# Combining attention parts inside the mixing stage, giving slabs back behind the evacuation, rounding T4 on GpSimd

## The chip, the cores and the metric

The kernel runs on one core of a Trainium2 chip. That core has a matrix engine (TensorE, PE in the profile), a vector engine (VectorE, DVE), an activation engine (ScalarE, ACT), a general engine (GpSimd, POOL) and a queue that issues transfers (SyncE, SP). Each engine works through its own instructions in order, and waits on semaphores for the others. The metric is the device time of one execution in microseconds; a kernel's time is the median of its runs.

## The reference

One layer of a hybrid encoder with 1024 channels runs on two batches of 512 tokens, in float32:

```python
xn = rmsnorm(x, norm1_g)
lru_x, lru_gate, q, k, v, gates = split(xn @ w_in)
xc = dwconv(lru_x); h = rglru(xc, forward) + rglru(xc, backward)
a_out = (gelu(lru_gate) * h) @ w_lru_out
# q, k: rmsnorm per head and rope; three groups of 8 heads, windows 128, 512, 2048, dilations 1, 4, 16
wts = softmax(lse of the three groups); o = sum(wts * out of the three groups)
b_out = o @ w_att_out
x = x + (sig(g_a) * a_out + sig(g_b) * b_out) @ w_o
up = rmsnorm(x, norm2_g) @ w_up;  gate, val = split(up)
x = x + (gelu(dwconv(gate)) * val) @ w_down
```

There are 1280 recurrent channels (10 tiles of 128), 512 columns of attention output after the groups are combined, and 3072 feed-forward channels (24 tiles, called f).

## The kernel before, in words

**Products.** Every float32 operand is split into a rounded part hi and a remainder lo, and each product is three matmuls (hi by hi, hi by lo, lo by hi) of 128x128 weights against 512 columns, `mm3`. Activations stay transposed in SBUF.

**The weight stream.** The weights of the whole program are one list of slabs, `specs`, in the order of use. An object `ws` moves along it at two points: SP loads a raw slab (128x512, four buffers `raw`), and `split_to` (L221 to L232) makes hi (ACT or DVE, L226 and L228) and lo (L231, on the engines of the list `lo_eng` in turn; V is DVE, G is POOL) in rings of eight. `ws.take` hands slabs to a product, `ws.done` gives their ring places back, `ws.adv(n)` writes the loads and splits of the next n slabs at that place of the program. Since each engine runs in order, the place of `ws.done` and `ws.adv` sets what stands ahead of what on ACT, DVE, POOL and SP. `defer(n, fn)` writes work n steps later.

**Stages**, in us of the profiled execution: norms and transposes; the first stage (to 424), columns of w_in for the recurrence (L), the output gates (G, stored as tanh in `sg_d`) and the first three gate columns (Y), with the recurrence's small blocks (`lru_slot`) in between; projections and attention (to about 1025), whose parts for 128 tokens and a head group go out to `num_d` with their maxima and sums; the other gate columns (to 1083), seven columns with two halves of 24 matmuls, each multiplied by the recurrence's h into y; the mixing of batch 0 (to 1179), the output product, the mixing and output product of batch 1, the second norm and the operands of a Strassen-Winograd form of the up product (to about 1390); up products (to 1848); down products (to the end).

**Combining.** Eight parts t of 128 tokens are combined, each from three groups. `comb_load` (L858) loads three 128x528 tiles, `combine` (L866) takes 13 operations of 128x8 on DVE, one exp on ACT (L874, with an activation table to load when the gelu's was there), three 128x512 multiplications on DVE (L883) and two additions on POOL (L885, L886). Parts 0 to 3 (batch 0) are transposed by PE (`o_transpose`, L891 to L898; L895 is the matmul); parts 4 to 7 (batch 1) go to DRAM `o_d`, stored from POOL's queue (L888), and are read again in the output product of batch 0. Before, all eight are combined in the gate columns i = 2 to 6 by the table `combs` (L914), up to two per column.

**Mixing.** `mix_tile` (L1002) makes one of eight output tiles of 128 channels: 30 matmuls of y and 12 of the attention output into a pair of PSUM banks, two pairs in turn. Its epilogue on DVE reads the halves with the gates tha and thb (L1018, L1019; `th_load` L994 loads them a tile ahead), adds them (L1020), and makes hi on ACT (L1021) and lo on DVE (L1022).

**Feed-forward.** The seven products of a tile f use operands B11, B21, T2, T1, T3, B22, T4. `batch0` (L1222) makes the first two; its results are copied to p1 (ACT, L1229) and added to g0 (DVE, L1234). `rest` (L1237) makes the other five in banks A and C: u (ACT copy L1248, or for f < 4 a DVE add L1246), p5 (ACT L1253 or DVE L1251), then T3, B22 and T4 continue in the same banks. `prod` (L1207, its matmuls L1214 to L1216) ends with `ws.done` and `ws.adv`, so the next slabs' loads, sums (DVE, L260) and splits are written ahead of the evacuation of this product. The operands T1 to T4 of batch 1 are made in four parts of 128 tokens by `sums_T` (L1130 to L1168): for T4 POOL makes two sums (L1145 is the helper's line), ACT rounds (L1166), POOL makes the remainder.

Of the kernel before, what the change touches and what calls it, by code (L numbers as in the profile page):

```python
# [11 lines left out]
F32 = mybir.dt.float32  # L12
F32R = mybir.dt.float32r
AF = mybir.ActivationFunctionType
ALU = mybir.AluOpType
# [99 lines left out]
def layer_kernel(ctx: ExitStack, tc: tile.TileContext, xs_in, norm1_g, w_in, conv_w, conv_b, lru_wa, lru_ba,  # L115
# [468 lines left out]
    for s, (typ, c) in enumerate(steps1):  # L584
        if s < 2:
            continue
        slabs = ws.take(2)
        ps = ps1.tile([128, 2, 512], F32, tag="m", bufs=2, name="ps")
# [33 lines left out]
    cm_a, ap = open_pool("att", side="right")  # L622
    lo_eng[0] = G

# [240 lines left out]

    def combine(t, cg):  # L866
        d = p3.tile([128, 3, 8], F32, tag="cd", bufs=2, name="cd")
        e = p3.tile([128, 3, 8], F32, tag="ce", bufs=2, name="ce")
        m = p3.tile([128, 8], F32, tag="cm", bufs=2, name="cm")
        V.tensor_tensor(out=m, in0=cg[0][:, 512:520], in1=cg[1][:, 512:520], op=ALU.max)  # L870
# [15 lines left out]
        G.tensor_tensor(out=cg[0][:, 0:512], in0=cg[0][:, 0:512], in1=cg[2][:, 0:512], op=ALU.add)  # L886
        if t >= 4:
            defer(1, lambda: G.dma_start(out=o_d[128 * (t - 4):128 * (t - 4) + 128, :], in_=cg[0][:, 0:512]))  # L888
        else:
            defer(1, lambda: o_transpose(t, cg[0], ps2, "tr"))  # L890
# [22 lines left out]
    ATT_DONE = 3  # L913
    combs = {2: (0,), 3: (1, 2), 4: (3, 4), 5: (5, 6), 6: (7,)}  # L914
    h_load(EARLY_Y)
# [156 lines left out]
    def o_phase(b, hook, orders):  # L1072
        for n, (kq, hlf) in enumerate(orders):
# [5 lines left out]
            ws.done("a", 4)  # L1079

    th_load(0, 0)
    ws.adv(8)
    for c in range(KD):
        mix_tile(0, c)
        if c == 3:
            load_acc(0)
            SP.dma_start(out=gain2, in_=norm2_g[0].partition_broadcast(128))
# [47 lines left out]
    def sums_T(i, pst):  # L1135
# [29 lines left out]
        yield  # L1165
        A.copy(out=hi("T4"), in_=t1)  # L1166
        sub(G, lo("T4"), t1, hi("T4"))
# [38 lines left out]

    def prod(ps, slab, op, start, free=True):  # L1207

        wh, wl = slab
        bh, bl = x2[op]  # L1210
        for k in range(4):
            a = wh[:, 128 * k:128 * k + 128]
            kw = dict(skip_group_check=True)
            PE.matmul(out=ps, lhsT=a, rhs=bh[:, k], start=(start and k == 0), stop=False, **kw)  # L1214
            PE.matmul(out=ps, lhsT=a, rhs=bl[:, k], start=False, stop=False, **kw)  # L1215
            PE.matmul(out=ps, lhsT=wl[:, 128 * k:128 * k + 128], rhs=bh[:, k], start=False, stop=(k == 3), **kw)  # L1216
        if free:
            ws.done("a", 1)
            ws.adv(pace[0])

# [3 lines left out]
    def batch0(f, nm="A", mid=None):  # L1224
# [3 lines left out]
        p1[f] = row("p1", 2)  # L1228
        A.copy(out=p1[f], in_=pa)  # L1229
        if mid:  # L1230
            mid()
        prod(pb, ws.take(1)[0], "B21", True)
        g0s[f] = row("g0", EARLY)
        V.tensor_tensor(out=g0s[f], in0=p1[f], in1=pb, op=ALU.add)  # L1234
        return pa

    def rest(f, pa, mid=None):  # L1237
# [9 lines left out]
        else:  # L1247
            A.copy(out=u2, in_=pa)  # L1248
        prod(pc, ws.take(1)[0], "T1", True)
        if early:  # L1250
            V.tensor_tensor(out=p5, in0=p1[f], in1=pc, op=ALU.add)  # L1251
        else:
            A.copy(out=p5, in_=pc)  # L1253
        prod(pa, ws.take(1)[0], "T3", False)
        if mid:
            mid()
        V.tensor_tensor(out=p5, in0=p5, in1=pa, op=ALU.add)
        prod(pc, ws.take(1)[0], "B22", False)
        V.tensor_tensor(out=u2, in0=u2, in1=pc, op=ALU.add)
        w = lambda j: vff[:, 24 * j + f:24 * j + f + 1]  # L1260
        gc = fp.tile([128, 2, S], F32, tag="gc", bufs=1, name="gc")
# [6 lines left out]
        act(out=gc, in_=gc, func=AF.Gelu_apprx_tanh)  # L1268
        prod(pa, ws.take(1)[0], "T4", False)
        V.tensor_tensor(out=gc[:, 1], in0=gc[:, 1], in1=p5, op=ALU.mult)  # L1270
        if early:
# [126 lines left out]
```

## Time and profile before

| | before |
| --- | --- |
| times, two runs | 2118.45 and 2120.14 us, median 2119.3 |
| profiled execution | 2119.48 us, span 2117.7, so 1.8 us lie around the span |
| PE busy | 2028.3 us, 96% of the span |
| DVE, ACT, POOL busy | 1320.9, 878.3, 669.1 us |
| granted TensorE clock, mean | 0.984 |
| DMA | 220.28 MB, mean 104 GB/s |

Times below are microseconds from the start of the span. A granted clock of 1.00 is 2.4 GHz, 0.50 is 1.2 GHz; a value between is a mixture over the stretch. In a row of a timeline the bracket tells how long the engine idled before it and which instruction ended that; several equal instructions in a row are one line with their number.

### The profile page before, as it was taken

Reading aid. Unit: us, or ns where it says so; the run is one execution under the profiler, and the core shown is the slowest. Engines: PE = TensorE matmul, PEld = TensorE weight load, DVE = VectorE, ACT = ScalarE, POOL = GpSimd, SP = SyncE. Lnnn points to the kernel's source line nnn. Section 1 sums busy time; section 2 is a strip of 40 time slices with the busy share of each in tenths; the row PEclk is TensorE's granted clock in tenths of the full one; section 3 lists DMA queues with packets and bytes.
Section 4 is the critical chain, followed back from the end, with each engine's and each line's share of the span. In section 5 each row is a group of like instructions: output and inputs, shape, how many; then the busy total and the mean of one; then the engine's idle time right before and its main releaser. Section 6 shows DMA issues by size and latency. Waiting matters only on the chain. (4 is left out here: it accounts for less than half of the span.)

```text
span 2117.7 us, 26439 instructions
## 1 busy us (share of the span) xinstructions
PE 2028.3 (96%) x9571; PEld 1708.6 (81%) x9571; DVE 1320.9 (62%) x1896; ACT 878.3 (41%) x1503; POOL 669.1 (32%) x562
## 2 busy tenths in 40 slices
PE   8999999899999999999979999877999999999999
PEld 6877777688899999998767888666888888788887
DVE  5589988736881673366675564666655555465555
ACT  4478888831442143125533332433444444421210
POOL 3111111025211522423343133442445544532421
PEclk9999999999999999999999999989999999999999
DMA  4444545431111111103547565312223332352322
GB/s 146 143 130 121 143 129 160 122 107 46 31 41 46 43 42 58 44 14 96 171 130 237 162 187 169 124 50 90 81 69 90 90 90 71 128 199 80 110 90 80
DMA packets 203776, 220.28 MB, mean 104 GB/s; under 512 B 28892, under 2 KB 148222, under 8 KB 203646
## 3 DMA queue, kind: packets, MB, share of 16 engines
q1 hardware_dynamic: 201278, 212.30, 32.4%
q0 software_dynamic: 2368, 6.29, 1.2%
q8 instruction: 75, 1.23, 0.2%
q14 instruction: 55, 0.45, 0.1%
HBM read 162.51 MB, written 50.79 MB: 101 GB/s over the span
## 5 line engine op out<-in xcount | busy, mean ns | idle before, releaser
L231 POOL TENSOR_TENSOR lo<-raw,hi 128x512 fp32r<-128x512 f32 (+1 forms) x252 | 344.1, 1377 | 661.8 <-ACT hi L228 559.7
L228 ACT CAST hi<-raw 128x512 fp32r<-128x512 f32 (+1 forms) x352 | 205.0, 606 | 322.6 <-PE psd L1351 152.8
L816 PE MATMUL ps<-hi,xh 128*128 128x512 f32 x576 | 252.3, 438 | 5.5 <-ACT gl L602 5.5
L817 PE MATMUL ps<-lo,xh 128*128 128x512 f32 x576 | 229.2, 398 | 0.0
L818 PE MATMUL ps<-hi,xl 128*128 128x512 f32 x576 | 228.8, 397 | 0.0
L152 PE MATMUL ps<-xh,hi 128*128 128x512 f32 x544 | 216.1, 397 | 0.3 <-DVE xc L404 0.3
L153 PE MATMUL ps<-xl,hi 128*128 128x512 f32 x544 | 214.0, 393 | 0.0
L154 PE MATMUL ps<-xh,lo 128*128 128x512 f32 x544 | 213.7, 393 | 0.0
L1352 DVE TENSOR_TENSOR accd<-accd,psd 128x512 f32<-128x512 f32 x192 | 130.0, 685 | 109.5 <-PE psd L1351 104.2
L816 PEld LDWEIGHTS ps<-hi,xh 128*128 128x128 f32 x576 | 156.6, 272 | 15.8 <-ACT gl L602 5.9
L817 PEld LDWEIGHTS ps<-lo,xh 128*128 128x128 f32 x576 | 158.8, 276 | 6.0
L818 PEld LDWEIGHTS ps<-hi,xl 128*128 128x128 f32 x576 | 156.8, 272 | 8.1
L1351 PE MATMUL psd<-hi,hp 128*128 128x512 f32 x384 | 149.4, 389 | 0.0
L1350 PE MATMUL psd<-lo,hp 128*128 128x512 f32 x384 | 149.4, 389 | 0.0
L1349 PE MATMUL psd<-hi,hp 128*128 128x512 f32 x384 | 149.4, 389 | 0.0
L716 ACT ACTIVATE p<-p,nm 128x128 f32<-128x128 f32 (+1 forms) x192 | 81.7, 427 | 144.2 <-DVE nm L714 143.8
L1214 PE MATMUL pfA<-T,hi 128*128 128x512 f32 x288 | 115.2, 400 | 19.1 <-ACT u L1248 14.1
L152 PEld LDWEIGHTS ps<-xh,hi 128*128 128x128 f32 x544 | 103.7, 191 | 23.9 <-issue 0.9
L638 DVE TENSOR_REDUCE ss<-sq 128x8 f32<-128x512 f32 x48 | 32.9, 685 | 142.4 <-ACT sq L635 142.4
L154 PEld LDWEIGHTS ps<-xh,lo 128*128 128x128 f32 x544 | 103.4, 190 | 22.4
L153 PEld LDWEIGHTS ps<-xl,hi 128*128 128x128 f32 x544 | 103.9, 191 | 21.5
L1216 PE MATMUL pfA<-T,lo 128*128 128x512 f32 x288 | 114.8, 399 | 0.9 <-POOL lo L231 0.9
(267 smaller groups left out, 4544.4 us busy)
## 6 DMA issues: line engine op xcount, KB each, us to landing
raw<-in_w_in_dram SPq DMA_DIRECT2D x144, 256.0 KB
raw<-in_w_up_dram SPq DMA_DIRECT2D x56, 256.0 KB
r<-in_w_up_dram SPq DMA_DIRECT2D x48, 256.0 KB
f_d<-gc SPq DMA_DIRECT2D x24, 512.0 KB
raw<-in_w_down_dram SPq DMA_DIRECT2D x48, 256.0 KB
hraw<-f_d SPq DMA_DIRECT2D x24, 512.0 KB
sg_d<-sgt SPq DMA_DIRECT2D x16, 512.0 KB
raw<-in_w_lru_out_dram SPq DMA_DIRECT2D x32, 256.0 KB
```

The lines of the kernel that those rows point to most:

```text
L152: PE.matmul(out=ps, lhsT=a, rhs=b, start=(k == 0), stop=False)
L153: PE.matmul(out=ps, lhsT=a, rhs=rl(k), start=False, stop=False)
L154: PE.matmul(out=ps, lhsT=wl(k), rhs=b, start=False, stop=(k == n - 1))
L228: A.copy(out=hi[:, 0:n], in_=r[:, 0:n])
L231: e.tensor_tensor(out=lo[:, 0:n], in0=r[:, 0:n], in1=hi[:, 0:n], op=ALU.subtract)
L816: PE.matmul(out=ps, lhsT=a, rhs=hi, start=(k == 0), stop=False)
L817: PE.matmul(out=ps, lhsT=a, rhs=lo, start=False, stop=False)
L818: PE.matmul(out=ps, lhsT=b, rhs=hi, start=False, stop=(k == KD - 1))
L1349: PE.matmul(out=ps, lhsT=hh[:, i, tl], rhs=w[0], start=(i == 0), stop=False)
L1350: PE.matmul(out=ps, lhsT=hh[:, i, tl], rhs=w[1], start=False, stop=False)
L1351: PE.matmul(out=ps, lhsT=hl[:, i, tl], rhs=w[0], start=False, stop=(i == 1))
L1352: V.tensor_tensor(out=acc[t][:, cl], in0=acc[t][:, cl], in1=ps, op=ALU.add)
```

## The change

It has four edits. The parts 4 to 7 are combined after tiles 1 to 4 of batch 0's mixing, in tiles called late that use the space of the norm's later operands; their loads stand on SP behind the gate loads of tiles 0 and 1, and their stores to `o_d` are issued by SP one tile after the combining. The parts 0 to 3 are combined one per gate column. In the feed-forward products `ws.done` and `ws.adv` are now a function `give`, called behind each product's evacuation. T4's rounding goes from ACT to POOL. In the last five steps of the first stage `lo_eng` alternates between DVE and POOL where it was DVE alone.

```diff
@@ -584,6 +584,8 @@
     for s, (typ, c) in enumerate(steps1):
         if s < 2:
             continue
+        if s == len(steps1) - 5:
+            lo_eng[:] = [V, G]
         slabs = ws.take(2)
         ps = ps1.tile([128, 2, 512], F32, tag="m", bufs=2, name="ps")
         main_mm(ps[:, 0], 0, slabs)
@@ -620,7 +622,7 @@
     cm_sb, ring_pool["b"] = open_pool("slabs_b")
     ws.open_ring("b")
     cm_a, ap = open_pool("att", side="right")
-    lo_eng[0] = G
+    lo_eng[:] = [G]
 
     msk = ap.tile([128, 768], F32, name="msk")
     rope = ap.tile([128, 12, 2, 16], F32, name="rope")
@@ -863,10 +865,10 @@
             cg.append(c)
         return cg
 
-    def combine(t, cg):
-        d = p3.tile([128, 3, 8], F32, tag="cd", bufs=2, name="cd")
-        e = p3.tile([128, 3, 8], F32, tag="ce", bufs=2, name="ce")
-        m = p3.tile([128, 8], F32, tag="cm", bufs=2, name="cm")
+    def combine(t, cg, small=None):
+        d, e, m = small or (p3.tile([128, 3, 8], F32, tag="cd", bufs=2, name="cd"),
+                            p3.tile([128, 3, 8], F32, tag="ce", bufs=2, name="ce"),
+                            p3.tile([128, 8], F32, tag="cm", bufs=2, name="cm"))
         V.tensor_tensor(out=m, in0=cg[0][:, 512:520], in1=cg[1][:, 512:520], op=ALU.max)
         V.tensor_tensor(out=m, in0=m, in1=cg[2][:, 512:520], op=ALU.max)
         for g in range(3):
@@ -884,9 +886,7 @@
                             op=ALU.mult)
         G.tensor_tensor(out=cg[0][:, 0:512], in0=cg[0][:, 0:512], in1=cg[1][:, 0:512], op=ALU.add)
         G.tensor_tensor(out=cg[0][:, 0:512], in0=cg[0][:, 0:512], in1=cg[2][:, 0:512], op=ALU.add)
-        if t >= 4:
-            defer(1, lambda: G.dma_start(out=o_d[128 * (t - 4):128 * (t - 4) + 128, :], in_=cg[0][:, 0:512]))
-        else:
+        if t < 4:
             defer(1, lambda: o_transpose(t, cg[0], ps2, "tr"))
 
     def o_transpose(t, src, pool, tag):
@@ -911,7 +911,7 @@
             hts[c, b] = t
 
     ATT_DONE = 3
-    combs = {2: (0,), 3: (1, 2), 4: (3, 4), 5: (5, 6), 6: (7,)}
+    combs = {2: (0,), 3: (1,), 4: (2,), 5: (3,)}
     h_load(EARLY_Y)
     for c in range(EARLY_Y, KR):
         i = c - EARLY_Y
@@ -1078,10 +1078,28 @@
                 hook(4 * n + i, i if n == 3 else None)
             ws.done("a", 4)
 
+    late = {}
+
+    def late_load(t):
+
+        r = x20p.tile([128, 2048], F32, name="late", tag=("B11h", "B11l", "B21h", "B21l")[t - 4], bufs=1)
+        cg = [r[:, 528 * g:528 * g + 528] for g in range(3)]
+        for g in range(3):
+            SP.dma_start(out=cg[g], in_=num_d[g][128 * t:128 * t + 128, :])
+        r3 = lambda ap: ap.rearrange("p (g h) -> p g h", g=3)
+        late[t] = cg, (r3(r[:, 1584:1608]), r3(r[:, 1608:1632]), r[:, 1632:1640])
+
     th_load(0, 0)
     ws.adv(8)
     for c in range(KD):
         mix_tile(0, c)
+        if c in (0, 1):
+            late_load(4 + 2 * c)
+            late_load(5 + 2 * c)
+        if 1 <= c <= 4:
+            combine(c + 3, *late[c + 3])
+        if 2 <= c <= 5:
+            SP.dma_start(out=o_d[128 * (c - 2):128 * (c - 2) + 128, :], in_=late[c + 2][0][0][:, 0:512])
         if c == 3:
             load_acc(0)
             SP.dma_start(out=gain2, in_=norm2_g[0].partition_broadcast(128))
@@ -1163,7 +1181,7 @@
         sub(G, t1, hi("B21"), t2)
         sub(G, t1, t1, lo("B21"), ALU.add)
         yield
-        A.copy(out=hi("T4"), in_=t1)
+        G.tensor_scalar(out=hi("T4"), in0=t1, scalar1=1.0, scalar2=1.0, op0=ALU.mult, op1=ALU.mult)
         sub(G, lo("T4"), t1, hi("T4"))
         yield
 
@@ -1204,7 +1222,11 @@
     g0s, p1 = {}, {}
     pace = [1]
 
-    def prod(ps, slab, op, start, free=True):
+    def give():
+        ws.done("a", 1)
+        ws.adv(pace[0])
+
+    def prod(ps, slab, op, start):
 
         wh, wl = slab
         bh, bl = x2[op]
@@ -1214,9 +1236,6 @@
             PE.matmul(out=ps, lhsT=a, rhs=bh[:, k], start=(start and k == 0), stop=False, **kw)
             PE.matmul(out=ps, lhsT=a, rhs=bl[:, k], start=False, stop=False, **kw)
             PE.matmul(out=ps, lhsT=wl[:, 128 * k:128 * k + 128], rhs=bh[:, k], start=False, stop=(k == 3), **kw)
-        if free:
-            ws.done("a", 1)
-            ws.adv(pace[0])
 
     bank = lambda nm: pf[nm].tile([128, 512], F32, tag=nm, bufs=2, name="pf" + nm)
     row = lambda nm, bufs=1: fp.tile([128, S], F32, tag=nm, bufs=bufs, name=nm)
@@ -1227,11 +1246,13 @@
         prod(pa, ws.take(1)[0], "B11", True)
         p1[f] = row("p1", 2)
         A.copy(out=p1[f], in_=pa)
+        give()
         if mid:
             mid()
         prod(pb, ws.take(1)[0], "B21", True)
         g0s[f] = row("g0", EARLY)
         V.tensor_tensor(out=g0s[f], in0=p1[f], in1=pb, op=ALU.add)
+        give()
         return pa
 
     def rest(f, pa, mid=None):
@@ -1246,17 +1267,21 @@
             V.tensor_tensor(out=u2, in0=p1[f], in1=pa, op=ALU.add)
         else:
             A.copy(out=u2, in_=pa)
+        give()
         prod(pc, ws.take(1)[0], "T1", True)
         if early:
             V.tensor_tensor(out=p5, in0=p1[f], in1=pc, op=ALU.add)
         else:
             A.copy(out=p5, in_=pc)
+        give()
         prod(pa, ws.take(1)[0], "T3", False)
         if mid:
             mid()
         V.tensor_tensor(out=p5, in0=p5, in1=pa, op=ALU.add)
+        give()
         prod(pc, ws.take(1)[0], "B22", False)
         V.tensor_tensor(out=u2, in0=u2, in1=pc, op=ALU.add)
+        give()
         w = lambda j: vff[:, 24 * j + f:24 * j + f + 1]
         gc = fp.tile([128, 2, S], F32, tag="gc", bufs=1, name="gc")
         for b, g in enumerate((g0s.pop(f), u2)):
@@ -1267,6 +1292,7 @@
                                    op0=ALU.mult, op1=ALU.add)
         act(out=gc, in_=gc, func=AF.Gelu_apprx_tanh)
         prod(pa, ws.take(1)[0], "T4", False)
+        give()
         V.tensor_tensor(out=gc[:, 1], in0=gc[:, 1], in1=p5, op=ALU.mult)
         if early:
             V.tensor_tensor(out=p5, in0=p1[f], in1=pa, op=ALU.add)
```

Three places show how the instructions move. Line numbers of the changed kernel are larger, from L864 on by 2, in the feed-forward by some 20. A name's ending counts the buffers.

SP's queue, from the weights of one mixing tile to the next (`raw` are weights, `tha` and `thb` the gates, `num_d` the parts in DRAM), at the gates of tile 1, before:

```order
L217 DMA raw<-in_w_att_out_dram 128x4x128
L217 DMA raw<-in_w_lru_out_dram 128x4x128 x2
L217 DMA raw<-in_w_lru_out_dram 128x2x128
L998 DMA tha<-sg_d 128x512
L998 DMA thb<-sg_d 128x512
L217 DMA raw<-in_w_att_out_dram 128x4x128
L217 DMA raw<-in_w_lru_out_dram 128x4x128 x2
L217 DMA raw<-in_w_lru_out_dram 128x2x128
L998 DMA tha<-sg_d 128x512
```

The same place now:

```order
L217 DMA raw<-in_w_att_out_dram 128x4x128
L217 DMA raw<-in_w_lru_out_dram 128x4x128 x2
L217 DMA raw<-in_w_lru_out_dram 128x2x128
L998 DMA tha<-sg_d 128x512
L998 DMA thb<-sg_d 128x512
L1088 DMA late<-num_d_63 128x528
L1088 DMA late<-num_d_64 128x528
L1088 DMA late<-num_d_65 128x528
L1088 DMA late<-num_d_63 128x528
L1088 DMA late<-num_d_64 128x528
L1088 DMA late<-num_d_65 128x528
L217 DMA raw<-in_w_att_out_dram 128x4x128
```

Six loads of late parts now stand between the gates of tile 1 and the weights behind them; six more stand behind the gates of tile 2.

DVE, in the mixing of batch 0, from one tile's epilogue (L1018 to L1022) over the remainders of the next weights (L231) to the next epilogue, before:

```order
L1018 SCALAR_TENSOR_TENSOR tha<-tha,ps 128x512
L1019 SCALAR_TENSOR_TENSOR thb<-thb,ps 128x512
L1020 TENSOR_TENSOR tha<-tha,thb 128x512
L1022 SCALAR_TENSOR_TENSOR ml<-tha,mh 128x512
L231 TENSOR_TENSOR lo<-raw,hi 128x512
L231 TENSOR_TENSOR lo<-raw,hi 128x256
L1018 SCALAR_TENSOR_TENSOR tha<-tha,ps 128x512
L1019 SCALAR_TENSOR_TENSOR thb<-thb,ps 128x512
```

Now, between the epilogue of tile 1 and that of tile 2, from the sum of the weights of a part to the first instructions of tile 2's epilogue (L883 and L885 are L881 and L883 of before; five rows of 128x8 operations stand ahead of these):

```order
L880 TENSOR_TENSOR late<-late 128x8
L881 RECIPROCAL late<-late 128x8
L883 TENSOR_TENSOR late<-late 128x8
L885 TENSOR_TENSOR late<-late 128x512
L883 TENSOR_TENSOR late<-late 128x8
L885 TENSOR_TENSOR late<-late 128x512
L883 TENSOR_TENSOR late<-late 128x8
L885 TENSOR_TENSOR late<-late 128x512
L231 TENSOR_TENSOR lo<-raw,hi 128x512
L231 TENSOR_TENSOR lo<-raw,hi 128x256
L1018 SCALAR_TENSOR_TENSOR tha<-tha,ps 128x512
L1019 SCALAR_TENSOR_TENSOR thb<-thb,ps 128x512
```

One whole part has moved in ahead of the weights' remainders and of the next tile's epilogue; so it is behind tiles 1 to 4.

ACT, around the copy u of f = 0 (L1248; `s` and `r` are sums and slabs of the up weights), before:

```order
L228 CAST hi<-r_11452 128x512
L228 CAST hi<-raw 128x512
L1166 CAST T_11016<-acc 128x4x128 x3
L228 CAST hi<-r_11454 128x512
L1248 COPY u_11670<-pfA 128x512
L228 CAST hi<-s_11702 128x512
L1253 COPY p_11671<-pfC 128x512
L228 CAST hi<-s_11701 128x512
```

The same place now (the copy is L1269, the copy of p5 L1275):

```order
L228 CAST hi<-r_11432 128x512
L228 CAST hi<-raw 128x512
L1269 COPY u_11650<-pfA 128x512
L228 CAST hi<-r_11434 128x512
L1275 COPY p_11651<-pfC 128x512
L228 CAST hi<-s_11683 128x512
L228 CAST hi<-s_11682 128x512
```

Three roundings of T4 (L1166) stood ahead of the copy and are gone from ACT, and each copy now stands ahead of the hi of the slab that its product gives way to.

## Rows read from the trace of the kernel before

**Rows 1.** Windows: busy us (instructions) per engine, granted clock, DMA share, GB/s
```profile
1040.00:1087.00 47.00, 36.05 (x157) 28.70 (x155) 38.27 (x97) 23.73 (x34) 19.62 (x14) 0.96 0.44 130
1087.00:1117.00 30.00, 21.02 (x85) 17.09 (x86) 21.68 (x46) 8.24 (x14) 14.17 (x13) 0.84 0.50 159
1117.00:1136.00 19.00, 19.00 (x77) 15.52 (x77) 12.83 (x16) 7.76 (x15) 7.81 (x6) 0.90 0.71 221
1155.00:1175.00 20.00, 20.00 (x90) 16.57 (x89) 8.63 (x13) 6.01 (x10) 5.18 (x4) 1.00 0.52 161
1390.00:1410.00 20.00, 11.84 (x40) 9.23 (x39) 9.82 (x9) 5.67 (x11) 13.80 (x10) 0.73 0.14 41
1510.00:1840.00 330.00, 330.00 (x1457) 273.27 (x1456) 181.68 (x224) 140.89 (x228) 168.68 (x123) 1.00 0.28 86
```

**Rows 2.** Waits of PE, 1000 to 1490 us: total, times, longest
```profile
PE pt L895 <- POOL cg L886: 8.0, 4, 3.3
PE pfB L1214 <- DVE g L1234: 4.8, 1, 4.8
...
PE pfC L1214 <- DVE p L1251: 2.7, 1, 2.7
PE pfA L1214 <- DVE u L1246: 2.4, 2, 1.5
```

**Rows 3.** Timeline of PE, columns and mixing: start, us, instruction, [idle <-releaser]
```profile
1060.91 0.66 PE L895 MATMUL pt<-ident,cg 128*128 128x128 f32 x4 [2.50 <-POOL cg L886]
...
1070.30 1.11 PE L895 MATMUL pt<-ident,cg 128*128 128x128 f32 x4 [3.26 <-POOL cg L886]
...
1087.18 0.80 PE L152 MATMUL ps<-yh,hi 128*128 128x512 f32 x1 [4.01 <-ACT gl L957]
...
1116.68 0.76 PE L152 MATMUL ps<-yh,hi 128*128 128x512 f32 x1 [8.80 <-DVE thb L1019]
```

**Rows 4.** Timeline of SP's queue before the third mixing tile
```profile
1112.50 0.32 SPq L998 DMA_DIRECT2D thb<-sg_d  x1
```

**Rows 5.** Timeline of DVE, one combining of attention parts
```profile
1044.98 0.15 DVE L870 TENSOR_TENSOR cm<-cg 128x8 f32<-128x8 f32 x1
...
1047.90 0.69 DVE L883 TENSOR_TENSOR cg<-cg,cd 128x512 f32<-128x512 f32 x1
...
1048.70 1.80 DVE L883 TENSOR_TENSOR cg<-cg,cd 128x512 f32<-128x512 f32 x1
```

**Rows 6.** Timeline of POOL, the same combining
```profile
1048.67 1.28 POOL L885 TENSOR_TENSOR cg<-cg 128x512 f32<-128x512 f32 x1 [5.36 <-DVE cd L881]
1050.64 1.59 POOL L886 TENSOR_TENSOR cg<-cg 128x512 f32<-128x512 f32 x1 [0.68 <-POOL cg L885]
```

**Rows 7.** Timeline of ACT, operand T4 and the first u copy
```profile
1395.99 0.62 ACT L1166 CAST T<-acc 128x512 fp32r<-128x512 f32 x1 [5.42 <-POOL acc L1145]
1400.55 0.62 ACT L1166 CAST T<-acc 128x512 fp32r<-128x512 f32 x1 [3.93 <-POOL acc L1145]
...
1401.59 0.58 ACT L1248 COPY u<-pfA 128x512 f32<-128x512 f32 x1
```

**Rows 8.** Timeline of PE: T3(0), the end of T4(0), T3(4)
```profile
1402.22 0.80 PE L1214 MATMUL pfA<-T,hi 128*128 128x512 f32 x1 [8.16 <-ACT u L1248]
...
1412.80 0.39 PE L1216 MATMUL pfA<-T,lo 128*128 128x512 f32 x1
...
1477.13 0.80 PE L1214 MATMUL pfA<-T,hi 128*128 128x512 f32 x1 [5.93 <-ACT u L1248]
```

**Rows 9.** Timeline of POOL, the last T4 remainder
```profile
1401.24 1.26 POOL L1145 TENSOR_TENSOR T<-acc,T 128x512 fp32r<-128x512 f32 x1 [0.73 <-ACT T L1166]
```

**Rows 10.** Groups of POOL by line and shape, whole span
```profile
L436 POOL TENSOR_SCALAR x<-xc 80x1024 fp32r<-80x1024 f32 x16 | 21.7, 1356 | 155.6 <-DMA xc<-xc_d 134.2 <-PE psg L458 21.5
```

**Rows 11.** Waits of PE, 380 to 440 us
```profile
PE ps L816 <- ACT gl L602: 5.5, 1, 5.5
PE psg L457 <- DVE u L468: 4.0, 1, 4.0
```

## The prediction, made before the changed kernel ran

> **What bounds the kernel now.** I read the windows first. From 1510 to 1840 us TensorE (PE) is busy for all of 330 us with 1457 recorded matmuls, 0.2265 us each at a granted clock of 1.00 [rows 1]: there nothing that another engine does sooner can help. So the change can only win where PE idles, or where it works at the lower of its two clock levels after idling. The list of PE's waits and its timeline say where those places are [rows 2, 3], at the mixing, in the first feed-forward products and at the end of the first stage; all that the change touches lies in them. Three edits concern this: **A**, four of the eight attention parts are combined during batch 0's mixing and not before it; **B and D**, the first feed-forward products (slabs given back behind the evacuation; T4 rounded by GpSimd, which is POOL); **C**, six lo subtractions go from VectorE (DVE) to POOL at the end of the first stage.
>
> **A, what goes.** Between the gate columns PE waits for POOL's last add of a part, four times, 8.0 us in all, of which 2.50 and 3.26 are the later two [rows 2, 3]. Then it waits 4.01 us for the last gate column and 8.80 us before the third mixing tile. This last one is a queue's: tile 0's second PSUM half can't be read until thb has been loaded, and SP issues that load only at 1112.50 [rows 4], since its wait is for a store of a combined part from POOL's queue. After the change DVE does one part per column, so the two later waits, the 4.01 and that store are gone: 2.50 + 3.26 + 4.01 + 8.80 = 18.6 us. The 8.0 − 2.50 − 3.26 = 2.2 us of the first two waits I leave, since those columns still have a part each. The idle stretches also cost clock. The clock of 0.84 over 1087 to 1117 and 0.90 over 1117 to 1136 [rows 1] is time at the lower level: 0.10 / 0.5 x 19 = 3.8 us of it in the second window, where PE is busy throughout, so half of that, 1.9, is lost; behind the 3.26 and the 4.01 waits the matmul rows at 1070.30 and 1087.18 are long (1.11 and 0.80 us), and the first window's 0.96 makes 0.04 / 0.5 x 47 = 3.8 us; some 2.6 us of work at half rate behind each wait lose 1.3 each. Sum for A: 18.6 + 4.5 = 23 us.
>
> **A, what it adds.** Each of mixing tiles 1 to 4 gets a part on DVE. One part holds DVE from 1044.98 to 1048.70 + 1.80 = 1050.50, 5.5 us [rows 5]. Without parts a tile takes DVE 8.63 us in 20 us (1155 to 1175), in the window with more to catch up 12.83 in 19 [rows 1]; a tile is 42 matmuls, 42 x 0.2265 = 9.5 us, so 4.1 to 6.4 us. Together 9.6 to 11.9 us of DVE in tiles of 9.5: over four tiles DVE falls behind by 0.4 to 9.6 us. PE feels it only when a PSUM pair isn't read in time: two pairs, so tile c + 2 starts a tile later, less the two reads, 0.7 us each by an operation of that shape [rows 5], 8.1 us of room. Stall 0 to 1.5 us; I take 0, as the mean of the two ends, 5, is inside the room. The twelve loads (128 x 528 x 4 bytes, 3.2 MB) stand on SP behind the gates of the next tile and ahead of its weights; the DMA share there was 0.50 to 0.71 [rows 1], so I take them as hidden by the slabs split ahead, with 0 to 4 us as bounds. The four POOL adds take 1.28 to 1.59 us [rows 6] with two lo subtractions behind them.
>
> The last multiplication of that part took 1.80 us where the one ahead of it took 0.69, and it ran while POOL's add ran [rows 5, 6]. The Trainium skill, "SBUF — State Buffer", section "SBUF: two separate sides", calls the pair of ports that DVE and GpSimd share an exclusive lock, held for a whole instruction; this pair of rows agrees, and no run here yet shows it in the mixing stage. By that rule every POOL instruction could stop one DVE instruction in full; the second rival works that out from rows.
>
> **B and D, the first f.** T3 of f = 0 starts 8.16 us late, in a stretch where PE works 11.84 of 20 us at a clock of 0.73 [rows 1], because the copy u leaves ACT only at 1401.59 [rows 7, 8]. ACT works in order, and ahead of that copy stand T4's roundings, which waited 5.42 and 3.93 us for POOL. D takes the roundings off ACT, so u is copied as soon as T2 ends. Late next is POOL: T4's last remainder ended at 1401.24 + 1.26 = 1402.50 [rows 9]. Two waits for ACT of 0.73 go, three roundings come at 0.68 each (half of 1.356 us for 1024 columns [rows 10]; up to 1.28, a two-operand add, if POOL has no better rate), and POOL meets DVE's T sums more, for which I take 1.8 us, one and a half operations delayed by 1.1 to 1.3 us each as in [rows 5]: 1402.50 − 1.46 + 2.04 + 1.8 = 1404.9. One lo (1.28) stands behind it for T4's slab: 1406.2. T4(0) then ends after 2.72 us and about 1.4 us of lower clock at 1410.4, against 1412.80 + 0.23 = 1413.0 before [rows 8]: **2.6 us** won of the 8.16. Bounds: 0 (POOL's chain 2.6 longer) to 8.16 + 2.7 (it is no bound at all, and T3's half rate, 0.80 us in its first row, goes as well).
> The wait of 4.8 us for g, at f = 3's first products, [rows 2] gets longer by about 1 us, since POOL's T4 work collides with DVE ahead of it. The waits on p (2.7) and u (2.4) at f = 2 and 3 [rows 2] are waits for DVE additions that stood behind the next slab's sums and lo; with B the addition comes first. I count 2.7 and the longer u wait (1.5) less 0.8 of a read still due, 3.4 us. At f = 4 T3 waits 5.93 us for u and then runs at half rate (0.80 us first row [rows 8]), 2.7 us lost: 8.6 us. The copy u now stands ahead of the next slabs' hi, but still behind one hi that waits for a load, and p behind two, so I leave 4.4 us: 4.2 won. From f = 5 on PE is full [rows 1] and the reordering is worth 0; its cover is PE's own work, with two PSUM banks per name. If a slab's lo came too late there, it would show as idle PE. One late evacuation near 1846 may give 0.8. Sum for B and D: 2.6 − 1 + 3.4 + 4.2 + 0.8 = **10 us**, bounds 1 and 18.
>
> **C.** PE waits 4.0 us for u and 5.5 for gl around the end of the first stage [rows 11]. DVE loses six subtractions of about 0.7 us there (0.69 for that shape [rows 5]), but the chain that ends last runs through the last blocks and the last gelu, of which I take a fifth of the 5.5: 1.2 us, bounds +1 (POOL's 1.28 us delays a slab) and −3.
>
> **The sum.** 23 + 10 + 1.2 = 34.2 us. The profiled execution took 2119.48 us (span 2117.7), 0.2 above the median of 2119.3: 2119.5 − 34.2 = **2085 us**. About 2%, 42 us, is what a measurement can tell from no change: under 2077 is faster by that, over 2162 slower.
>
> **Rivals.**
> *POOL is not in the way* (0.18): roundings and sums don't collide, the first f wins its bound, C its 3 and the two small column waits go too: 34 + 8 + 1.8 + 2.2 = 46 less 34.2, so 12 more: **2073**. For: ACT's waits of 5.42 and 3.93 were waits for POOL alone [rows 7]. Against: it is POOL's chain all the same.
> *DVE bounds the mixing* (0.18): POOL has two adds and two lo per tile; if each holds a DVE operation back by 1.1 us (1.80 − 0.69), the tile costs DVE 10.1 + 4.4 = 14.5 us, 5 over the tile, 20 in four, less 8 of room: 12 us stall, **2097**. The lock rule of that Trainium skill page would bring this.
> *T4 only changes the engine waited for* (0.05): B and D win 1, not 10: **2094**.
> *Slower* (0.04): SP holds it back. The weights of tile c + 2 stand behind loads and stores of the late parts, and their buffers come free only when POOL's lo, queued behind the two adds, is done. If a part ends more than one tile (9.5 us) after its tile's epilogue, each of tiles 2 to 5 stops as the third tile did: 8.80 plus about 5 of lower clock, 4 x 13.8 = 55: **2140**. Against: 1.5 us of stall at most by the rows above.
> The forecast's own case, 2078 to 2093, has 0.55. The range of 2066 to 2106 takes in the first two rivals with their bounds. Faster by over 2%: 0.2, from the first rival and the edge of the forecast; within 2%: 0.77; slower by over 2%: 0.03, the far end of the last rival.
>
> **What the profile will show.** Right: mixing starts near 1076, its third tile near 1095 without a gap; T3(0) follows T1 without a wait, and T4(0) waits 3 to 6 us for POOL; 1510 to 1840 stays full. Wrong: PE waits for DVE's thb operation or POOL's lo between tiles 2 and 6 (second or last rival), no wait at T4(0) (first), idle PE in the later f (B costs something).

## The result, and the profile after

The changed kernel took 2095.8 us (2095.2 and 2096.45), before 2119.3: a ratio of 0.9889 with a 95% interval of 0.9847 to 0.9932, 23.5 us faster. The forecast was 2085 with a range of 2066 to 2106. The time lies inside the range, 11 us above the forecast, outside the forecast's own case of 2078 to 2093 and between the rivals at 2094 and 2097. The profiled execution's span is 2093.4 us, 24.3 less than before.

Where the 24.3 us went shows in the starts of the stages. Each number is the start of the first matmul of that stage in PE's timeline, in us; a stage's length is the difference between two columns.

| kernel | projections | mixing, batch 0 | output product | mixing, batch 1 | feed-forward | down | end |
| --- | --- | --- | --- | --- | --- | --- | --- |
| before | 424.2 | 1087.2 | 1175.8 | 1225.6 | 1351.6 | 1852.6 | 2117.7 |
| the change | 427.2 | 1077.9 | 1156.5 | 1209.5 | 1335.7 | 1827.1 | 2093.4 |
| change in the stage ahead | +3.0 | -12.3 | -10.0 | +3.2 | +0.2 | -9.6 | +1.2 |

So A is worth 12.3 + 10.0 - 3.2 - 0.2 = 18.9 us (the forecast had 23), the feed-forward 9.6 less 1.2 given back in the down products (10), and the first stage, where C is, became 3.0 us longer (1.2 shorter). These are two single profiles; how far such starts scatter is said at the experiments.

PE's waits of the changed kernel between 1030 and 1480 us (total, times, longest), which answer to [rows 2, 3, 8]:

```profile
PE pfB L1236 <- DVE g L1254: 6.5, 1, 6.5
PE pt L895 <- DMA ost<-o_d: 3.5, 2, 3.3
PE pfA L1236 <- POOL T L1184: 2.7, 1, 2.7
PE pfA L1236 <- ACT u L1269: 2.5, 1, 2.5
PE pt L895 <- POOL cg L888: 2.2, 2, 1.3
PE ps L152 <- DVE thb L1019: 2.1, 1, 2.1
```

The 4.01 and 8.80 us before and in the mixing, the later two waits for a part, and the 8.16 us at T3(0) are gone. Three waits are new or longer: 2.1 at the eighth and last mixing tile (tile 7, as tiles are numbered from 0; the expectations below call it the seventh), 3.3 for the load of a part into its tile ost, and 6.5 for g, which was 4.8. T4 now waits for POOL (2.7, with 0.9 and 0.9 more in its first matmuls).

Windows of the changed kernel, with the columns of [rows 1]: the last gate columns, the four mixing tiles with a part, the start of the output product, the first feed-forward products, the later ones:

```profile
1054.00:1078.00 24.00, 23.23 (x109) 19.33 (x110) 17.61 (x43) 12.29 (x19) 12.80 (x10) 1.00 0.40 124
...
1097.00:1145.00 48.00, 47.84 (x212) 39.29 (x210) 40.65 (x92) 13.24 (x26) 20.76 (x15) 1.00 0.65 217
1145.00:1170.00 25.00, 19.62 (x89) 15.83 (x90) 18.46 (x23) 8.36 (x15) 8.31 (x7) 1.00 0.69 221
1380.00:1400.00 20.00, 15.46 (x57) 11.56 (x56) 13.41 (x12) 7.57 (x11) 14.48 (x11) 0.83 0.11 35
1500.00:1810.00 310.00, 310.00 (x1369) 256.86 (x1368) 190.46 (x213) 131.71 (x212) 162.73 (x113) 1.00 0.27 82
```

From 1054 to 1145 PE has its full clock and hardly idles. DVE is busy 40.65 of 48 us in the tiles with parts. From 1500 on PE is as full as before: the reordering neither won nor cost there.

DVE's timeline of one tile with a part, from the epilogue's last operation (L1022) of tile 1 to that of tile 2, and POOL's beside it:

```profile
1100.34 0.69 DVE L1022 SCALAR_TENSOR_TENSOR ml<-tha,mh 128x512 fp32r<-128x512 f32 x1 [0.70 <-ACT mh L1021]
...
1103.87 0.69 DVE L885 TENSOR_TENSOR late<-late 128x512 f32<-128x512 f32 x1
...
1104.68 1.80 DVE L885 TENSOR_TENSOR late<-late 128x512 f32<-128x512 f32 x1
1106.40 2.12 DVE L231 TENSOR_TENSOR lo<-raw,hi 128x512 fp32r<-128x512 f32 x2
...
1109.75 1.72 DVE L1020 TENSOR_TENSOR tha<-tha,thb 128x512 f32<-128x512 f32 x1
1112.17 0.69 DVE L1022 SCALAR_TENSOR_TENSOR ml<-tha,mh 128x512 fp32r<-128x512 f32 x1 [0.70 <-ACT mh L1021]
```

```profile
1104.65 1.28 POOL L887 TENSOR_TENSOR late<-late 128x512 f32<-128x512 f32 x1 [5.56 <-DVE late L883]
1106.61 1.62 POOL L888 TENSOR_TENSOR late<-late 128x512 f32<-128x512 f32 x1 [0.68 <-PE ps L153]
1108.20 2.72 POOL L231 TENSOR_TENSOR lo<-raw,hi 128x512 fp32r<-128x512 f32 x2
```

A tile takes DVE 1112.17 - 1100.34 = 11.83 us, against PE's 9.5, at the upper end of the 9.6 to 11.9 of the prediction. Three operations in it are long: the third multiplication (1.80, not 0.69), a remainder of half the width inside the 2.12, and the sum L1020 (1.72). Each begins beside one of POOL's. The whole trace of the kernel before shows the same pair: 366 of DVE's TENSOR_TENSOR operations of 128x512 read two operands in SBUF; the 246 that began with no arithmetic of POOL running took 0.70 us at most, and of the 120 that began beside one 116 took over 0.80. Another 468 of that shape read one operand from PSUM; 148 of them began beside POOL, and none took over 0.70. Then the lag adds up. The eighth tile stops, and later the output product waits for the first part of batch 1, whose load SP issues only at 1160.43, behind weight loads that wait for buffers. PE's two stops, and SP's queue:

```profile
1146.91 0.47 PE L152 MATMUL ps<-yh,hi 128*128 128x512 f32 x1 [2.08 <-DVE thb L1019]
...
1165.47 0.66 PE L895 MATMUL pt<-ident,ost 128*128 128x128 f32 x4 [3.35 <-DMA ost<-o_d]
```

```profile
1156.37 3.54 SPq L219 DMA_DIRECT2D raw<-in_w_o_dram  x4
1159.95 0.42 SPq L1115 DMA_DIRECT2D yst<-y_d  x1
1160.43 0.42 SPq L1118 DMA_DIRECT2D ost<-o_d  x1
```

At the end of the first stage the same pair of engines shows what C did. DVE and POOL of the changed kernel, then DVE before, at the same product of a block (L479) and its two scans (L487):

```profile
369.63 2.36 DVE L479 TENSOR_TENSOR u<-u,w 80x1024 f32<-80x1024 f32 x1
372.02 3.31 DVE L487 TENSOR_TENSOR_SCAN u<-thr,u 80x512 f32<-80x512 f32 x2
```

```profile
369.61 1.30 POOL L231 TENSOR_TENSOR lo<-raw,hi 128x512 fp32r<-128x512 f32 x1 [3.52 <-PE psg L458]
371.35 1.79 POOL L231 TENSOR_TENSOR lo<-raw,hi 128x512 fp32r<-128x512 f32 x1 [0.44 <-ACT hi L228]
```

```profile
369.65 1.22 DVE L479 TENSOR_TENSOR u<-u,w 80x1024 f32<-80x1024 f32 x1
370.90 2.34 DVE L487 TENSOR_TENSOR_SCAN u<-thr,u 80x512 f32<-80x512 f32 x2
```

Two subtractions moved to POOL take 2 x 0.69 us off DVE, but its product and scans beside them take 5.67 us where they took 3.56, 2.1 more. These scans make u, on which the rest of the stage hangs. C by itself (below) shows it too: there the two pairs of scans took 4.37 and 3.06 us where they took 2.34 each.

### The profile page after: what moved, and what is told of

The parts are those of the page before. It is cut to its first block, busy times and chain, and to the rows that moved or that the text cites. A ratio compares the mean times of both kernels' runs of the same rounds, so it can differ in the third digit from the quotient of the medians.

```text
span 2093.4 us, 26372 instructions
## 1 busy us (share of the span) xinstructions
PE 2022.4 (97%) x9571; PEld 1704.3 (81%) x9571; DVE 1344.9 (64%) x1890; ACT 867.4 (41%) x1493; POOL 692.8 (33%) x568
## 5 line engine op out<-in xcount | busy, mean ns | idle before, releaser
L231 POOL TENSOR_TENSOR lo<-raw,hi 128x512 fp32r<-128x512 f32 x258 | 354.8, 1387 | 615.3 <-ACT hi L228 549.6
```

Of the source, the lines that this page charges most:

```text
L231: e.tensor_tensor(out=lo[:, 0:n], in0=r[:, 0:n], in1=hi[:, 0:n], op=ALU.subtract)
```

## The experiments

All ratios are against the kernel before, run on the same chip in turn. The first four do one edit each.

**A alone** (the kernel before, with the parts of the change in the mixing and `combs` of one per column).

> Only edit A (parts 4 to 7 in the mixing, one part per column before it). Theory from the two traces: A is worth what the shifts of PE's starts say, 18.6 us (the operand stage begins 16.1 us sooner, though the projections began 2.5 us later), so about 2100.7 us, with DVE taking 11.8 us per mixing tile, a PE wait of about 2 us at the seventh tile and one of about 3 us for the first load of ost. Rival: the mixing's late waits come from the other edits' shift of the weights, then A alone gives the 23 us of the prediction, 2096.

Measured: 2102.3 us, ratio 0.9917 (0.9904 to 0.9931), 16.9 us faster. The projections began at 423.5 and the feed-forward at 1330.7, 20.2 us less than before between the two. The wait at the eighth tile was 3.0 us. No wait for ost is listed: SP issued that load 1.15 us after the output product began (1156.65 against 1155.50), in the change 3.9 us after (1160.43 against 1156.52). The sum of the theory holds within the interval, one of its two waits came, and the rival of 23 us does not hold.

**B alone** (diff shortened; the calls of `give` behind the evacuations are as in the change).

```diff
-        if free:
-            ws.done("a", 1)
-            ws.adv(pace[0])
+    def give():
+        ws.done("a", 1)
+        ws.adv(pace[0])
...
```

> Only edit B (slabs given back behind the evacuation). Theory: B takes away the waits on p and u at f = 2, 3 and part of f = 4, but not the 8.16 us at T3(0), which stands behind T4's roundings on ACT: 5 to 7 us, about 2113. Rival: the reordering gets the 8.16 us as well, 2105; or it delays splits in the later f and gives 0, 2119, with PE idle between 1510 and 1840.

Measured: 2110.6 us, ratio 0.9965 (0.9952 to 0.9977), 8.6 us faster; the feed-forward took 490.9 us, not 501.0, and the down products 1.0 more. PE's longest waits between 1340 and 1490 us:

```profile
PE pfA L1218 <- ACT u L1251: 9.2, 2, 7.5
PE pfB L1218 <- DVE g L1236: 4.8, 1, 4.8
```

T3(0) still waits 7.5 us for u. What B wins is at f = 2 to 4: the 2.7 for p are gone, and the 5.93 for u at f = 4 became 1.7, with 1.6 for p. From T2 of f = 1 to the first product of f = 5 it won 8.0 us, more than the 5 to 7 expected.

**C alone.**

```diff
+        if s == len(steps1) - 5:
+            lo_eng[:] = [V, G]
```

> Only edit C (six lo subtractions from DVE to POOL at the end of the first stage). Theory from the traces: it costs 2.5 to 3 us, since a raw buffer is freed later by POOL's slower subtraction, SP's load of the next weights is later and ACT's gelu stands behind that slab's hi: 2121.8. Rival: the 3 us later start of the projections was not C's (a load that landed late by chance), then 2119 or the 1.2 us gain of the prediction, 2118.

Measured: 2123.8 us, ratio 1.0024 (1.0014 to 1.0034): slower by 3 to 7 us. C costs. The expected way, through the raw buffers, was wrong in its first link: in the change SP's loads are late because the store of u ahead of them is late (380.83, before 378.67), and u is late from the scans shown above.

**D alone.**

```diff
-        A.copy(out=hi("T4"), in_=t1)
+        G.tensor_scalar(out=hi("T4"), in0=t1, scalar1=1.0, scalar2=1.0, op0=ALU.mult, op1=ALU.mult)
```

> Only edit D (T4 rounded on POOL). Theory: the copy u leaves at once, the 8.16 us at T3(0) go, but T4(0) waits for POOL's chain 4 to 5 us, and the wait for g before it grows by 1.6: a gain of 1 to 3 us in all, 2117. Rival: T4(0) isn't bound by POOL, and D alone is worth 6 us or more, 2113.

Measured: 2120.4 us, ratio 1.0006 (0.9998 to 1.0015): no change. PE's longest waits between 1340 and 1490 us:

```profile
PE pfB L1214 <- DVE g L1234: 6.4, 1, 6.4
...
PE pfA L1214 <- POOL T L1166: 4.7, 1, 4.7
```

The 8.16 us at T3(0) are gone, 4.7 (with 1.2 and 0.9 behind it) appear at T4(0), and g costs 1.6 more. 8.2 became 8.4: the wait changed its engine.

**The change without C.**

> The change without edit C. Theory: C's 2 to 4.6 us come back, 2092 (between 2091 and 2093.5), and the projections begin near 424 us. Rival: C costs nothing beside A, B and D, 2096.

Measured: 2092.5 us, ratio 0.9872 (0.9858 to 0.9887), 3.3 us under the change. The change has only two runs, both above all four of these; its interval (0.9847 to 0.9932) takes in this ratio, so it is C alone, with nine runs, that settles that C costs. One profile would not: among the twelve kernels without C the projections began between 423.2 and 426.5 us, in C alone at 425.4.

**A and B, without C and D.**

> Edits A and B alone (neither C nor D: T4 rounded by ACT). Theory that D gives nothing anywhere, since it only moves the wait at f = 0 from T3 (for ACT's copy u) to T4 (for POOL): the same as without C, 2092, with a wait of 7 to 8 us at T3(0) and none at T4(0). Rival: D is worth 4 us once B is there (the sum of the four single edits, -16.9 - 8.6 + 4.6 + 1.2 = -19.7, leaves 3.8 of the change's 23.5 unexplained): 2096.

Measured: 2093.2 us, ratio 0.9875 (0.9861 to 0.989), the same as without C. D gives nothing beside B either: T3(0) waits 7.5 us here, and with D T4(0) waits 4.4 and g 1.6 more. A alone and B alone, 16.9 + 8.6, add to the 25.5 of this kernel. That all four single edits add to 19.7 and the change gave 23.5 is then within what these medians scatter.

**Parts behind tiles 1, 3, 5, 6**, without C, as in the next ones (diff shortened; the stores to `o_d` move with the parts).

```diff
-        if 1 <= c <= 4:
-            combine(c + 3, *late[c + 3])
+    PART = {1: 4, 3: 5, 5: 6, 6: 7}
...
+        if c in PART:
+            combine(PART[c], *late[PART[c]])
...
```

> Without C, and with the four late parts behind tiles 1, 3, 5 and 6 and not 1 to 4. Theory that DVE's 11.8 us per tile with a part, against PE's 9.5, add up over four tiles in a row: spread out, DVE catches up in between, PE's wait of 2 to 3 us at the seventh tile goes, and with it some lower clock: 2089. Rival: that wait is the late load of weights behind the four loads of acc on SP, then it stays and the time is as without C, 2092.

Measured: 2096.5 us, ratio 0.9891 (0.9877 to 0.9906): 4 us slower than without C, where 3 faster were expected. The wait at the eighth tile is gone though the four loads of acc stayed behind tile 3, so these loads don't make it by themselves; it takes DVE's lag (what the loads add to it is said with the prediction's terms below; acc are the rows of x to which the output product is added). But the one PE wait left between 1070 and 1200 us is this, and SP's queue shows why:

```profile
PE pt L893 <- DMA ost<-o_d: 6.4, 1, 6.4
```

```profile
1148.41 10.58 SPq L219 DMA_DIRECT2D raw<-in_w_o_dram  x4
1159.03 0.42 SPq L1102 DMA_DIRECT2D o_d<-late  x1
1159.51 0.42 SPq L1115 DMA_DIRECT2D yst<-y_d  x1
1159.98 0.49 SPq L1118 DMA_DIRECT2D ost<-o_d  x1
```

Four weight loads hold SP for 10.58 us, since their buffers come free behind POOL's and DVE's remainders, which the later part delays. The load of a part that was long done stands behind them.

**Additions of late parts on DVE.**

```diff
-        G.tensor_tensor(out=cg[0][:, 0:512], in0=cg[0][:, 0:512], in1=cg[1][:, 0:512], op=ALU.add)
+        E = V if small else G
+        E.tensor_tensor(out=cg[0][:, 0:512], in0=cg[0][:, 0:512], in1=cg[1][:, 0:512], op=ALU.add)
...
```

> Without C, and the two additions of each late part on DVE and not on POOL. Theory that DVE and POOL stop each other where both read two SBUF operands: the third multiplication falls from 1.80 to 0.69 us and the 128x256 remainder from 1.52 to 0.48, so although DVE gets two additions (1.4 us) more, a tile with a part takes it 11.0 to 11.3 us and not 11.84, and PE's wait at the seventh tile shrinks by 2 us or more: 2090. Rival: no such stop, DVE's tile grows to 13.2 us and PE waits 4 to 6 us more: 2097.

Measured: 2094.3 us, ratio 0.9879 (0.9861 to 0.9897): no difference from without C. DVE's timeline of a tile (the multiplications L883, the first addition L886, the two remainders, the end of the epilogue), and one row of POOL:

```profile
1125.07 1.79 DVE L883 TENSOR_TENSOR late<-late 128x512 f32<-128x512 f32 x1
...
1127.77 0.69 DVE L883 TENSOR_TENSOR late<-late 128x512 f32<-128x512 f32 x1
1128.38 0.68 DVE L886 TENSOR_TENSOR late<-late 128x512 f32<-128x512 f32 x1
...
1129.71 1.02 DVE L231 TENSOR_TENSOR lo<-raw,hi 128x512 fp32r<-128x512 f32 x2
...
1136.21 1.35 DVE L1021 SCALAR_TENSOR_TENSOR ml<-tha,mh 128x512 fp32r<-128x512 f32 x1 [3.56 <-ACT mh L1020]
```

```profile
1125.02 1.29 POOL L231 TENSOR_TENSOR lo<-raw,hi 128x512 fp32r<-128x512 f32 x1 [7.53 <-ACT hi L228]
```

The third multiplication fell to 0.69 and the pair of remainders from 2.12 to 1.02, as the theory of the stop said. But now the first multiplication takes 1.79, beside a remainder on POOL that used to run elsewhere. In the two tiles ahead of this one, 12.12 us each, two operations were stopped and not one, so the two additions were not paid for. This tile took 13.88, as DVE waited 3.56 us for mh, the rounded half that ACT makes (0.70 in the tiles ahead); its own work was the 11.0 us expected. PE waited 5.1 us at the eighth tile. The mechanism held, the sum did not.

**Transposing the parts from the late tiles** (diff shortened; the store to `o_d` and the load ost are left out too, and the tiles B11 and B21 are opened after the last transpose).

```diff
-            o_transpose(n - 1, ostage.pop(n - 1), ps3, "t")
+            o_transpose(n - 1, late[n + 3][0][0], ps3, "t")
```

> Without C, and PE transposes parts 4 to 7 straight from the late tiles: no store to o_d and no load ost. Theory that in the change the output product of batch 0 waits for a part that has long been combined, because SP issues its load ost behind weight loads: the 2.25 and 0.48 us waits for ost go, and some 1 us of lower clock behind them: 2089. The wait of 2.4 us at the seventh mixing tile stays. Rival: the transposes then wait for the last parts themselves, or the output product for its weights, and nothing is won: 2092.

Measured: 2088.1 us, ratio 0.985 (0.9835 to 0.9865), 4 us under the change without C, though the five runs lie between 2083.8 and 2092.4 and the two intervals overlap a little. The only PE wait listed between 1070 and 1200 us is the eighth tile's, 1.7 us, and in the profiles the output product took 48.7 us, and without C 52.2.

**The same, parts behind 1, 3, 5, 6.**

> As before, with the parts behind tiles 1, 3, 5 and 6. Theory that both waits of the mixing stage are then gone, DVE's (which spreading took away) and the load's (which spreading alone made 6.4 us): 2086.5, with no wait of PE over 0.5 us from the third gate column to the end of batch 0's output product. Rival: the part behind tile 6 comes late for its transpose and PE waits 2 us or more there: 2089.

Measured: 2089.5 us, ratio 0.9855 (0.9842 to 0.9869): no gain over the last one. PE's waits between 1070 and 1200 us:

```profile
PE pt L893 <- DVE acc L1068: 1.0, 1, 1.0
PE pt L893 <- DVE ol L896: 0.6, 1, 0.6
```

The eighth tile's wait went, and 1.6 us at the transposes came.

**The same, with g ahead of the sums.**

```diff
-        if mid:
-            mid()
         prod(pb, ws.take(1)[0], "B21", True)
         g0s[f] = row("g0", EARLY)
         V.tensor_tensor(out=g0s[f], in0=p1[f], in1=pb, op=ALU.add)
         give()
+        if mid:
+            mid()
```

> As before, and the additions into g of the first feed-forward tiles stand ahead of the operands' sums on DVE (the sums are written behind the second product, not between the two). Theory that PE's wait of 6.5 us for g, which D made 1.6 us longer, is only the order on DVE: it goes with its lower clock, and part comes back as a longer wait at T2(0): 2082. Rival: the sums are the bound of the stage and every microsecond comes back at T2 or T4: 2086 to 2089.

Measured: 2082.7 us, ratio 0.982 (0.9806 to 0.9833), the fastest of all: 13 us under the change. The wait for g is gone; its longest waits from 1030 to 1480 us are now

```profile
PE pst L1153 <- ACT T L1172: 6.0, 2, 4.1
PE pfA L1231 <- DVE p L1275: 2.8, 2, 2.2
```

Of the 6.5 us for g, 4.1 came back at a transpose that waits for a bank of sums, but the waits at T4(0) fell from 6.3 us to 3.4. In all, T2 of f = 1 begins 5.9 us sooner in the stage than without this edit. In this profile the feed-forward took 489.6 us, and in the five without this edit but with D and without C 491.4 to 495.4.

**The same, parts behind 1, 2, 4, 5.**

> As before, with the parts behind tiles 1, 2, 4 and 5, so that two in a row are followed by a tile without one and the last is done a tile sooner. Theory: DVE's lag of 2.3 us per tile with a part stays inside the 8 us that two PSUM pairs give, so no wait at the seventh tile, and the transposes find their parts (0.96 and 0.36 us of wait go): 2081. Rival: the lag was not what held the transposes, 2082.7 as with 1, 3, 5 and 6.

Measured: 2088.7 us, ratio 0.9852 (0.9835 to 0.987): 6 us slower than the last, where 2 faster were expected. PE's waits between 1070 and 1200 us:

```profile
PE pt L893 <- DVE acc L1068: 1.7, 1, 1.7
PE ps L152 <- DVE thb L1017: 1.6, 1, 1.6
PE pso L1064 <- POOL lo L231: 1.2, 1, 1.2
```

The eighth tile waits again, and the output product now also waits for its weights' remainders. No part stands behind tile 3, so that DVE could catch up there, but it waited in tile 4's epilogue:

```profile
1134.33 1.36 DVE L1020 SCALAR_TENSOR_TENSOR ml<-tha,mh 128x512 fp32r<-128x512 f32 x1 [7.50 <-ACT mh L1019]
```

```profile
1133.15 0.62 ACT L228 CAST hi<-raw 128x512 fp32r<-128x512 f32 x1 [9.65 <-DMA raw<-in_w_att_out_dram]
```

ACT makes mh behind a hi whose weights SP issued at 1124.04, right behind the four loads of acc and one of gain; with the parts behind 1, 3, 5 and 6 this wait is 0.70. That those loads delayed the weights is inferred from the order in the queue; loading acc at another place was not tried. Between the two profiles, 6.1 us apart, the mixing took 1.8 us more and the output product 2.5 more; the first stage, which is the same code, took 2.2 more, and the feed-forward and down products together 0.3 less.

## Why the prediction was right, and where its terms were off

The time came inside the range and on the forecast's side, but 11 us above the forecast. The range owes its upper end to the second rival, so that the time lies in it says little for the forecast's own sum. Of its signs, the starts of the mixing (1077.9 for 1076) and of the third tile (1097.1 for 1095, without a gap), the missing wait at T3(0), the wait at T4(0) and the full PE later on came as told; so did the second rival's, PE waiting for thb, one tile later than named. By its steps:

- **A, what goes: right.** To the start of the mixing 12.3 us, where 2.50 + 3.26 + 4.01 and 1.3 of lower clock make 11.1. In the mixing 10.0, where 8.80 and 1.9 + 1.3 of lower clock make 12.0, less the new wait of 2.08.
- **A, what it adds: mis-sized.** "Stall 0 to 1.5 us; I take 0" took the middle between 9.6 and 11.9 us per tile. It was 11.8, and at tile 4 12.7, as mh waited on ACT behind a hi whose weights SP had issued (at 1126.88) behind acc's loads:

```profile
1136.72 1.36 DVE L1022 SCALAR_TENSOR_TENSOR ml<-tha,mh 128x512 fp32r<-128x512 f32 x1 [2.59 <-ACT mh L1021]
```

```profile
1135.54 0.62 ACT L228 CAST hi<-raw 128x512 fp32r<-128x512 f32 x1 [8.60 <-DMA raw<-in_w_att_out_dram]
```

  The lag from tile 1's L1022 (1100.34) to tile 5's (1149.19) is 48.85 - 4 x 9.5 = 10.8 us, over the room of 8.1 by 2.7; PE waited 2.08. Of the lag 2.59 - 0.70 = 1.9 us are this wait behind acc's loads, so without it most of the 2.08 would have gone (an estimate from these rows). And a second cost had no term: the output product's first part, 3.35 us. The sum had followed SP for the twelve loads and not for the loads ost behind the weights. Both come from DVE's lag; the second reached SP through the buffers that DVE frees, for which SP's weight loads waited 10.5 us between 1140 and 1168.
- **The second rival's mechanism was the one at work**, at a smaller price. It asked for 1.1 us per POOL operation in a tile, four of them; three stops were measured (1.80 - 0.69, 2.12 - 1.02, 1.72 - 0.69), 3.2 us. Its 10.1 us for a tile without stops, which the text doesn't derive, was too much: 11.83 - 3.2 leaves 8.6, under PE's 9.5, so but for acc's loads the lag is all POOL's (an estimate from these rows). The Trainium skill, "SBUF — State Buffer", section "SBUF: two separate sides", says of the pair of ports that DVE and GpSimd share that whichever instruction starts first keeps it to its end and the other waits in full. The runs agree: the stop left the third multiplication when POOL's additions left, and turned up at another operation as soon as POOL ran there.
- **B and D: right in sum, but not D's share.** In the change's trace T1 to T4 of f = 0 took 19.3 us and not 21.9, the 2.6 of the forecast, and the longer wait for g (6.47; it stands at f = 2's second product, not at f = 3's) cost 1.6 and not 1. From T2 of f = 1 to the first product of f = 5 it won 7.4 (forecast 7.6). At the last f it won 1.2 (0.8), which the down products gave back: 8.4 us against 10. But B alone won 0.8 up to T2 of f = 1 and 8.0 from there on, and D alone was 1.1 behind at that T2: what D took from T3(0) came back at T4(0) and at g. The rival "T4 only changes the engine waited for" holds for D, in D alone and beside B; it is not for D that the sum came out. POOL's rounding took 0.94 to 1.06 us in the rows of the last three, not the 0.68 of the sum, inside its bounds:

```profile
1387.74 0.94 POOL L1184 TENSOR_SCALAR T<-acc 128x512 fp32r<-128x512 f32 x1
1388.77 1.57 POOL L1163 TENSOR_TENSOR T<-acc,T 128x512 fp32r<-128x512 f32 x1
```

  T4's chain on POOL ended at 1388.77 + 1.57 = 1390.3; the stage began 15.9 us sooner, so on the clock of the kernel before that is 1406.2, 1.3 us behind the forecast's 1404.9.
- **C: wrong in sign.** "I take a fifth of the 5.5" counted six subtractions less on DVE. It left out that each, on POOL, can stop DVE for longer (1.0 to 1.1 us) than it took there (0.69). The bound of +1 was too near: C costs 3 to 7 us alone, and some 3.3 beside the other edits.

The forecast's sum was 23 + 10 + 1.2 = 34.2; the one of the two profiles is 18.9 + 8.4 - 3.0 = 24.3. What remains open is why A alone gave 20.2 us in its own profile and 16.9 in the median; its four runs lie 5.8 us apart.

## What to carry to other kernels

Before moving an elementwise operation from DVE to POOL, look at what DVE runs beside it: if that reads two operands in SBUF, the move costs DVE nearly as much as a POOL operation takes (here 1.0 to 1.1 us for one of 1.28), wherever it lands. Where a wait is taken from an in-order engine, look for the next operand of the same product; if another engine's chain makes it, the wait only changes its name, and one run with that edit alone shows it. A short result that goes out and comes back through a transfer queue waits for all that stands in the queue; if it still lies in SBUF, read it there.

## What the runs showed of the hardware that was not expected

- A product and two scans on DVE of 80 partitions took 5.67 us beside two POOL subtractions and 3.56 without them; a 128x512 multiplication took 1.80 or 0.69.
- An operation with one tensor operand on POOL took 0.62 us for 128x512 (at 1352.97) when DVE was waiting, and 0.94 to 1.06 when it was not.
- Of the kernels with the same first stage, the start of the projections scattered by 3.3 us between profiles (423.2 to 426.5), more than some of the edits are worth.
